# A hybrid attention and convolution layer: each modulation block's product in one group of sixteen matmuls, four weight buffers, and a reordered stage list

## The chip, the cores and the metric

The kernel runs on one core of a Trainium2 chip. The metric is the device time of one execution in microseconds (us). Three runs of the kernel before gave 747.54, 747.73 and 748.13 us, a median of 747.73.

The engines are named as in the profile: PE (TensorE, matmuls and transposes; PEld its weight loads), DVE (VectorE), ACT (ScalarE), POOL (GpSimd) and SP (the engine that issues nearly all the transfers).

## The reference

One layer of a diffusion model for 128 context tokens and 512 latent tokens (640 in all), model width 1024, all in float32:

```
mod = silu(cond) @ w_ada + b_ada            # (1, 6 * 1024): sh1, sc1, g1, sh2, sc2, g2
h = rms(x, norm_mix) * (1 + sc1) + sh1
q, k, v, gb, gc, u = split(h @ w_in)        # 512, 128, 128, 512, 512, 512 columns
attn   = softmax attention, 8 q heads, 2 kv heads, head size 64, rotary positions;
         latent queries see all 640 keys, context queries the 128 context keys
y_conv = gb * conv3(gc * u)
x = x + g1 * (concat(rms(attn), rms(y_conv)) @ w_out)
h2 = rms(x, norm_ffn) * (1 + sc2) + sh2
x = x + g2 * ((silu(gate) * up) @ w_down)   # gate, up = h2 @ w_gate_up, width 2816
```

There are two conditions: `c` for the latent tokens and `c_ctx` for the context tokens. Outputs are x of both kinds of token and k and v of the context tokens.

## The kernel before

Large products keep float32 accuracy by splitting each operand into a high and a low part (names ending in h and l or H and L) and summing three products: high by high, high by low, low by high. Activations are held with the contraction on partitions, 8 tiles of 128.

The program has four stages: the opening (norms, first modulation, the input projection), which ends near 80 us; attention together with the convolution's products, to about 251 us; the output projection with the second norm, to about 300 us; and the feed-forward part to the end.

**The stage list.** In the second stage the string `SEQ` sets the order in which steps are written out, and on PE, ACT, DVE and SP instructions run in that order but for small priorities. The entries are: `k`, `K`, `q`, `Q` (split, then turn a tile's keys or queries; `kv_mm`, `k_turn`, `q_split`, `q_turn`), `a`, `t`, `o` (scores, turn and output of context attention), `Sn.h`, `Tn.g`, `On.g` (`att_s`, `att_t`, `att_o`: scores, turn, and output of unit n, of 16), `r` (an rms), and `F1`, one piece of the filler.

A unit's scores (L835) go into one PSUM buffer "s". DVE takes their maximum (nsr L841), ACT the exponential (pr L845), and one of the two halves is scaled on ACT (L849), the other on DVE. PE then turns them (L862) and multiplies by v (L879). After two units of a head group, `att_add` sends the 64 partitions that must change place through two transfers (es, L894 and L895, 64 KB in all) and adds what comes back on DVE (of, L900 and L901).

**The filler.** Its 84 pieces are 72 convolution pieces and 12 modulation pieces, one modulation piece after every six convolution pieces. A convolution product (`conv_mm`, L723 to L725) accumulates 8 tiles in three pieces of nine matmuls for each half of the 640 tokens. Its PSUM buffer is one of three with the tag "c", which the modulation shares.

**The modulation.** The columns of `w_ada` for g1, sh2 and sc2 are six blocks of 512 (`ADA`). For each, `cond_mm` (L394) multiplies eight tiles of the condition by the weights; tile k writes the 32 PSUM partitions k % 4, so four tiles run side by side. The sum over the four is made later: for sh2 and sc2 by four transposes (L446) and a reduction (modt L448), for g1 by a matmul with `selT` (L785). One `cond_mm` is two instructions in the profile. The two lines between which a piece ends are

```
if h == 1:
    yield
```

so a block is two pieces with four products each, and the transposes of one block stand at the start of the next block's first piece, or, for the last block, in the out-projection. Weights of a block come in four loads of 512 KB (aw) into two buffers (`AWB`). `W` issues the next loads as soon as their buffers are free, in one order with all other weights (wf), on SP.

**The output projection** begins with the context tile's products (ph L155 to L157) behind the last entry of `SEQ`. Two lines of work on DVE run in it: wl L252 scales and splits w_out, aacc L1041 and L1043 forms the last modulation, g2.

Of the kernel before, what the change touches and what calls it, by code (L numbers as in the profile page):

```python
# [37 lines left out]
XB = 3  # L38
SEQ = ('c0 k1 q4 k4 C0 k0 K4 Q4 a0 q0 F1 k2 K0 a1 t0 k3 t1 K1 o0 F1 Q0 o1 K2 K3 q1 F1 S0.0 F1 F1 F1 S0.1 F1 '
# [10 lines left out]
GCUT = [0, 6, 12, 17, 22]  # L50
GB = 3
SOP = [20, 0]
# [20 lines left out]
BPL = 1500  # L73
AP0 = 60
MXP = [300, 200, 0, 0, 0]
AWB = 2
AO = 6
SOON = 150
SOW = -300
# [12 lines left out]
def build(ctx, tc, x_prompt, x_sample, c, cache_k, cache_v, c_ctx, norm_mix, norm_ffn, w_ada, b_ada,  # L92
# [27 lines left out]
    def T(tag, shape, dt=F32, bufs=1):  # L120
        seq[0] += 1
        return pools[where.get(tag, "A")][1].tile(list(shape), dt, tag=tag, bufs=bufs, name=f"{tag}_{seq[0]}")

    def PB(shape=(P, 512), dt=F32, tag="t"):
        seq[0] += 1
        if kept.get(tag):
            w = kept[tag].pop()
            n = 1
            for y in shape[1:]:
                n *= y  # L130
            w = w[:, :n] if tag != "s" else w
            if tag != "s" and len(shape) > 2:
                names = "abc"[:len(shape) - 1]
                w = w.rearrange("p (" + " ".join(names) + ") -> p " + " ".join(names), **dict(zip(names, shape[1:])))
            return w
        return pools["psum"][1].tile(list(shape), dt, tag=tag, bufs=pbufs[tag], name=f"p{tag}_{seq[0]}")
# [10 lines left out]
    def early(n):  # L147
        return tc.high_priority(n)
# [72 lines left out]
    def load(e, later=False):  # L221
# [4 lines left out]
        a, b = src.shape[1], src.shape[2]  # L226
        wf = T("aw", (P, a, b), F32, AWB) if ring == "a" else T("wf", (P, a, b), F32, WFB)
        sp.dma_start(wf, src)
# [30 lines left out]
    def W(key):  # L259
        p = place[key]  # L260
        while not in_pre[0] and stream_at[0] < len(order):
            nxt = order[stream_at[0]][0][0]
            ahead = AO if nxt == "o" else AOP if nxt in ("g", "u", "op") else AHEAD
            if stream_at[0] > p + ahead or order[stream_at[0]][2] > phase[0]:
                break
            load_next()
        assert order[p][5] is not None, key
        return order[p][5]
# [123 lines left out]
    def cond_mm(out, k, w):  # L392
        g = k % 4
        pe.matmul(out[CG * g:CG * (g + 1)], cp[:, k], w, start=(k < 4), stop=(k >= KD - 4), skip_group_check=True)  # L394
# [16 lines left out]
    def mod_evict(i, f0, n, ps_sc, ps_sh):  # L411

        no = (V_MIX, V_FFN)[i]
        bo = (0, 24)[i]
        if ps_sc is not None:
            tmp = ps_sc
            dve.tensor_tensor(tmp, ps_sc, vec[:, no + f0:no + f0 + n].unsqueeze(2).to_broadcast([P, n, 2]), ALU.mult)
            dve.tensor_tensor(modA[i][:, f0:f0 + n, :], tmp,
                              nb[:, i, f0:f0 + n].unsqueeze(2).to_broadcast([P, n, 2]), ALU.add)
        if ps_sh is not None:  # L420
            dve.tensor_tensor(modB[i][:, f0:f0 + n, :], ps_sh,
                              vec[:, bo + f0:bo + f0 + n].unsqueeze(2).to_broadcast([P, n, 2]), ALU.add)
# [19 lines left out]
    def mod_sum(res, n, tag):  # L442

        tp = PB((P, n, P), tag=tag)
        for i in range(n):
            pe.transpose(tp[:, i], res[:, i * P:(i + 1) * P], ident)  # L446
        out = T("modt", (P, n, 2), F32, 2)
        dve.tensor_reduce(out, tp.rearrange("p i (g c) -> p i c g", c=CG)[:, :, 0:2], AX.X, ALU.add)  # L448
        return out
# [317 lines left out]
    def ada_all():  # L767
        for sec, j in ADA:
            rp = PB(tag="c")
            for h in range(4):  # L770
                w = W(("ada", sec, j, h))
                for i in range(2):
                    cond_mm(rp, 2 * h + i, w[:, i])
                if h == 1:
                    yield
            res = T("rs5", (P, 512))
            with early(RSP) if RSP else ExitStack():
                act.activation(res, rp, AF.Copy)
            if sec == 2:
                sp.dma_start(res[2:3], b_ada[0:1, sec * D + j * 512:sec * D + (j + 1) * 512])  # L780
            yield
            if sec == 2:
                for cc in range(2):
                    ps = PB(tag="c")
                    pe.matmul(ps, selT[:, cc], res, start=True, stop=True)  # L785
                    act.activation(g1[cc][:, j * 512:(j + 1) * 512], ps, AF.Copy)
            else:
                ps = mod_sum(res, 4, "c")
                if sec == 4:
                    mod_evict(1, 4 * j, 4, ps, None)  # L790
                else:
                    mod_evict(1, 4 * j, 4, None, ps)

    ada_gen = ada_all()

    def ada_some(n):
# [171 lines left out]
    def rms_of(t):  # L968
        if t == CTX or t >= 0:
# [5 lines left out]
             "a": ctx_s, "t": ctx_t, "o": ctx_o, "r": att_rms}  # L975
    for x in SEQ.split():
        if "." in x:
# [120 lines left out]
    for j in range(2):  # L1098
        cols = slice(j * 512, (j + 1) * 512)
        for n, t in enumerate(TORD):  # L1100
            cc = 1 if t == CTX else 0
            c0 = t * P + (2 if t == CTX else 0)
# [230 lines left out]


tile_hymba = with_exitstack(build)

_INS = ["x_prompt", "x_sample", "c", "cache_k", "cache_v", "c_ctx", "norm_mix", "norm_ffn", "w_ada", "b_ada",
# [44 lines left out]
```

## Time and profile before

| | |
|---|---|
| median of three runs | 747.73 us (747.54 to 748.13) |
| the profiled execution's own time | 747.58 us |
| its span, first to last instruction | 745.8 us |
| mean granted TensorE clock | 0.999 |
| PE busy | 729.5 us, 98% |
| DVE busy | 529.8 us, 71% |
| ACT busy | 375.6 us, 50% |
| transfers | 84.50 MB, 113 GB/s on average |

The own time holds the span and 1.78 us around it. A matmul's busy time overlaps the next one's, so the distance from start to start tells what it costs PE, and a PE that is busy all of a window may still have room. A bracket behind a row of the timeline, [0.95 <-DVE modt L448], gives the idle time before the instruction and whose instruction ended it. The modulation groups (L394, weights aw) run from 94.0 to 249.7 us.

### The profile page before, as it was taken

How to read it: one execution, taken by the hardware profiler on the slowest of the kernel's cores; microseconds unless marked ns; L12 is line 12 of the kernel's file. 1: busy time of each engine (PE TensorE's matmuls, PEld its weight loads, DVE VectorE, ACT ScalarE, POOL GpSimd, SP SyncE). 2: the span in 40 equal slices, each digit the busy share in tenths (PEclk: the TensorE clock that was granted, in tenths of full speed). 3: DMA queues.
4: the chain of work that ended last, by engine and by line, in shares of the span. 5: the costliest groups of instructions: out<-in, count | busy, mean ns of one | idle time of the engine just before them, and what ended most of it. 6: DMA issues, size and time to landing. Idle time of an engine off the chain costs nothing.

```text
span 745.8 us, 11640 instructions
## 1 busy us (share of the span) xinstructions
PE 729.5 (98%) x4556; PEld 657.5 (88%) x4556; DVE 529.8 (71%) x905; ACT 375.6 (50%) x701; POOL 48.6 (7%) x85
## 2 busy tenths in 40 slices
PE   7999899999999999999999999999999999999997
PEld 5568878988998887899998799998899998899986
DVE  5668878685666797888869767864668765677653
ACT  5357877676766544765552135552135541354510
POOL 2403201002010210000000000000000000000000
PEclk9999999999999999999999999999999999999999
DMA  9985133523424363032336314224014132123312
GB/s 288 294 248 165 43 113 104 167 93 117 152 92 147 109 225 114 26 89 57 114 97 195 89 31 112 76 95 142 28 57 113 57 113 86 57 75 96 105 65 85
DMA packets 101387, 84.50 MB, mean 113 GB/s; under 512 B 3502, under 2 KB 81650, under 8 KB 101332
## 3 DMA queue, kind: packets, MB, share of 16 engines
q1 hardware_dynamic: 100980, 83.39, 36.6%
q8 instruction: 36, 0.59, 0.4%
q0 software_dynamic: 352, 0.37, 0.3%
q14 instruction: 19, 0.16, 0.1%
HBM read 79.68 MB, written 2.75 MB: 111 GB/s over the span
## 4 chain that ended last, share of the span: by engine, by line
PE 85%; DVE 6%; DMA 3%; ACT 3%; issue 2%; POOL 1%; SPq 0%; ACTq 0%; DVEq 0%; POOLq 0%
PE pf L155 19%; PE pf L156 19%; PE pf L157 19%; PE pc L723 3%; PE pc L725 3%; PE pc L724 3%; PE pt L862 3%; PE po L879 2%; PE ps L835 2%; PE pc L394 2%; PE ph L156 1%; PE ph L157 1%; PE ph L155 1%; DMA es<-t 1%; DMA af<-in_w_ada_dram 1%
## 5 line engine op out<-in xcount | busy, mean ns | idle before, releaser
L151 ACT ACTIVATE wh<-wf 128x1024 fp32r<-128x1024 f32 (+1 forms) x68 | 65.7, 969 | 107.3 <-PE pf L157 67.0
L152 DVE TENSOR_TENSOR wl<-wf,wh 128x1024 fp32r<-128x1024 f32 (+1 forms) x58 | 69.2, 1195 | 59.2 <-ACT wh L151 45.2
L155 PE MATMUL pf<-B,wh 128*128 128x320 f32 x288 | 89.1, 309 | 0.0
L157 PE MATMUL pf<-B,wl 128*128 128x320 f32 x288 | 89.1, 309 | 0.0
L156 PE MATMUL pf<-B,wh 128*128 128x320 f32 x288 | 89.0, 309 | 0.0
L155 PE MATMUL pf<-wh,gT 128*128 128x512 f32 (+1 forms) x225 | 86.9, 386 | 0.0
L155 PE MATMUL pf<-T,wh 128*128 128x320 f32 x280 | 86.7, 310 | 0.0
L156 PE MATMUL pf<-wl,gT 128*128 128x512 f32 (+1 forms) x225 | 86.5, 385 | 0.0
L156 PE MATMUL pf<-T,wh 128*128 128x320 f32 x280 | 86.5, 309 | 0.0
L157 PE MATMUL pf<-T,wl 128*128 128x320 f32 x280 | 86.5, 309 | 0.0
L157 PE MATMUL pf<-wh,gT 128*128 128x512 f32 (+1 forms) x225 | 86.5, 384 | 0.0
L151 ACT ACTIVATE wh<-sx 128x1024 fp32r<-128x1024 f32 x40 | 42.4, 1060 | 61.7 <-DVE sx L206 22.9
L152 DVE TENSOR_TENSOR wl<-sx,wh 128x1024 fp32r<-128x1024 f32 x40 | 49.0, 1225 | 28.5 <-ACT wh L151 24.9
L723 PE MATMUL pc<-hH,wh 128*128 128x320 f32 x192 | 61.0, 318 | 0.9 <-DVE modt L448 0.9
L725 PE MATMUL pc<-hH,wl 128*128 128x320 f32 x192 | 59.3, 309 | 0.0
L724 PE MATMUL pc<-hL,wh 128*128 128x320 f32 x192 | 59.3, 309 | 0.0
L157 PEld LDWEIGHTS pf<-B,wl 128*128 128x128 f32 x288 | 54.1, 188 | 0.1
L155 PEld LDWEIGHTS pf<-B,wh 128*128 128x128 f32 x288 | 54.1, 188 | 0.1
L156 PEld LDWEIGHTS pf<-B,wh 128*128 128x128 f32 x288 | 54.1, 188 | 0.1
L155 PEld LDWEIGHTS pf<-T,wh 128*128 128x128 f32 x280 | 52.5, 188 | 0.5 <-ACT pf L1241 0.3
L156 PEld LDWEIGHTS pf<-T,wh 128*128 128x128 f32 x280 | 52.6, 188 | 0.0
L157 PEld LDWEIGHTS pf<-T,wl 128*128 128x128 f32 x280 | 52.5, 188 | 0.0
(302 smaller groups left out, 1669.4 us busy)
## 6 DMA issues: line engine op xcount, KB each, us to landing
wf<-in_w_gate_up_dram SPq DMA_DIRECT2D x44, 512.0 KB, 4.1
aw<-in_w_ada_dram SPq DMA_DIRECT2D x24, 512.0 KB, 4.3
wf<-in_w_down_dram SPq DMA_DIRECT2D x20, 512.0 KB, 4.2
wf<-in_w_in_dram SPq DMA_DIRECT2D x18, 512.0 KB, 5.8
af<-in_w_ada_dram SPq DMA_DIRECT2D x32, 256.0 KB, 6.4
x<-in_x_sample_dram SPq DMA_DIRECT2D x8, 512.0 KB, 6.2
wf<-in_w_out_dram SPq DMA_DIRECT2D x8, 512.0 KB, 3.5
wf<-in_w_ada_dram SPq DMA_DIRECT2D x8, 512.0 KB, 3.9
```

The lines of the kernel that those rows point to most:

```text
L151: act.activation(hi, src, AF.Copy)
L152: dve.tensor_tensor(lo, src, f32(hi), ALU.subtract)
L155: pe.matmul(out, lh, rh, start=start, stop=False, skip_group_check=more)
L156: pe.matmul(out, lh, rl, start=False, stop=False, skip_group_check=more)
L157: pe.matmul(out, ll, rh, start=False, stop=stop, skip_group_check=more)
L394: pe.matmul(out[CG * g:CG * (g + 1)], cp[:, k], w, start=(k < 4), stop=(k >= KD - 4), skip_group_check=True)
L723: pe.matmul(acc, wh[:, k], hH[k][:, c0:c0 + n], start=(k == 0), stop=False)
L724: pe.matmul(acc, wh[:, k], hL[k][:, c0:c0 + n], start=False, stop=False)
L725: pe.matmul(acc, wl[:, k], hH[k][:, c0:c0 + n], start=False, stop=(k == KD - 1))
L835: pe.matmul(s2[:, g, :320], q, kk[:, v, P + g * 320:P + (g + 1) * 320], start=(i == 0), stop=(i == 1))
L862: pe.transpose(tp[:, i, h], u[3][h][:, kt * P:(kt + 1) * P], ident)
L879: pe.matmul(ov, w, x[:, i].rearrange("p a q -> p (a q)"), start=(g == 0 and i == 0 and n == 0), stop=(last and i == len(kts) - 1 and n == 1))
```

## The change

A block's modulation product becomes one piece: all eight `cond_mm` and the ACT copy of the result (`rs5`). The turn, or for g1 the two matmuls with `selT`, gets a piece of its own. The pieces stay 84 in number, and 12 of them modulation. `AWB` goes from 2 to 4. In `SEQ`, `K0` moves from before `a1` to behind `o0 F1`, `q1` from before `S0.0` to behind `S0.1 F1`, some thirty others by one to three places, and the last `F1` comes to stand behind `O15.2`. Line numbers from 774 on are smaller by one or two in the changed kernel (L835 becomes L834, L862 L861, L879 L878, L894 L893, L785 L783).

```diff
-SEQ = ('c0 k1 q4 k4 C0 k0 K4 Q4 a0 q0 F1 k2 K0 a1 t0 k3 t1 K1 o0 F1 Q0 o1 K2 K3 q1 F1 S0.0 F1 F1 F1 S0.1 F1 '
+SEQ = ('c0 k1 q4 k4 C0 k0 K4 Q4 a0 q0 F1 k2 a1 t0 k3 t1 K1 o0 F1 K0 Q0 o1 K2 K3 F1 S0.0 F1 F1 F1 S0.1 F1 q1 '
...
-AWB = 2
+AWB = 4
...
     def ada_all():
         for sec, j in ADA:
             rp = PB(tag="c")
             for h in range(4):
                 w = W(("ada", sec, j, h))
                 for i in range(2):
                     cond_mm(rp, 2 * h + i, w[:, i])
-                if h == 1:
-                    yield
             res = T("rs5", (P, 512))
...
                 else:
                     mod_evict(1, 4 * j, 4, None, ps)
+            yield
```

PE at the first group. Names are tile_number; the first block's product is pc_285 before, pc_278 after. Before:

```order
L835 MATMUL ps_282_1246<-KB_169_730,qT_263_1142 128x320 x2
L394 MATMUL pc_285_1258<-aw_179_756,cp_5_85 32x512 x2
L394 MATMUL pc_285_1258<-aw_227_961,cp_5_85 32x512 x2
L723 MATMUL pc_292_1278<-hH0_51_193,wh_165_715 128x320
L724 MATMUL pc_292_1278<-hL0_59_201,wh_165_715 128x320
L725 MATMUL pc_292_1278<-hH0_51_193,wl_166_716 128x320
```

After:

```order
L834 MATMUL ps_275_1229<-KB_169_730,qT_263_1142 128x320 x2
L394 MATMUL pc_278_1241<-aw_179_756,cp_5_85 32x512 x2
L394 MATMUL pc_278_1241<-aw_227_961,cp_5_85 32x512 x2
L394 MATMUL pc_278_1241<-aw_282_1248,cp_5_85 32x512 x2
L394 MATMUL pc_278_1241<-aw_283_1252,cp_5_85 32x512 x2
L723 MATMUL pc_298_1295<-hH0_51_193,wh_165_715 128x320
```

The block's second half, which ran at 112.57 us before, now stands behind its first, ahead of the next scores, S1.0.

PE at the last block's start, near 237 us. pc_675 is the fifth block's turn, pc_677 the sixth block's product, pt_692 a turn of scores. Before:

```order
L725 MATMUL pc_662_3002<-hH7_58_200,wl_605_2731 128x320
L446 MATMUL pc_675_3073<-ident_3_77,rs5_646_2923 128x128 x4
L394 MATMUL pc_677_3082<-aw_644_2915,cp_5_85 32x512 x2
L394 MATMUL pc_677_3082<-aw_645_2919,cp_5_85 32x512 x2
L862 MATMUL pt_692_3123<-ident_3_77,pr_633_2876 128x128
L862 MATMUL pt_692_3123<-ident_3_77,pr_649_2933 128x128
L723 MATMUL pc_695_3130<-hH0_51_193,wh_642_2911 128x320
```

After:

```order
L861 MATMUL pt_674_3070<-ident_3_77,pr_654_2949 128x128
L394 MATMUL pc_677_3082<-aw_611_2748,cp_5_85 32x512 x2
L394 MATMUL pc_677_3082<-aw_612_2752,cp_5_85 32x512 x2
L394 MATMUL pc_677_3082<-aw_678_3083,cp_5_85 32x512 x2
L394 MATMUL pc_677_3082<-aw_679_3085,cp_5_85 32x512 x2
L861 MATMUL pt_693_3129<-ident_3_77,pr_639_2892 128x128
L861 MATMUL pt_693_3129<-ident_3_77,pr_654_2949 128x128
L723 MATMUL pc_696_3136<-hH0_51_193,wh_609_2744 128x320
```

The turn that stood ahead of the group has gone to a place some seventy rows earlier, and the second half of the group has come from behind the last convolution product, some seventy rows later.

SP in the middle of the second stage: L228 a weight load, L894 and L895 (L893 and L894 after) the two transfers of es, t2 what they send. Before:

```order
L895 DMA es_515_2298<-t2_485_2154 64x2x128
L228 DMA aw_530_2375<-in_w_ada_dram 128x2x512
L228 DMA aw_531_2379<-in_w_ada_dram 128x2x512
L228 DMA wf_683_3095<-in_w_out_dram 128x2x512
L894 DMA es_561_2520<-t2_546_2437 64x2x128
```

After:

```order
L228 DMA aw_535_2389<-in_w_ada_dram 128x2x512
L228 DMA aw_536_2393<-in_w_ada_dram 128x2x512
L228 DMA aw_606_2734<-in_w_ada_dram 128x2x512
L228 DMA aw_607_2738<-in_w_ada_dram 128x2x512
L228 DMA wf_683_3095<-in_w_out_dram 128x2x512
L893 DMA es_561_2518<-t2_552_2453 64x2x128
```

Ahead of es_561 stand four loads of a block's weights in place of two.

18 rows, old and new, of the table SEQ are left out of this document.

## The prediction

> **What bounds the kernel now.** I read the page first, for the engine that carries the time. The profiled execution took 747.58 us by its own clock, 745.8 us of it the span, so 1.78 us lie around the span and are taken as unchanged. The median of the three runs is 747.73 us, 0.15 us above the profiled one.
>
> ```profile
> span 745.8 us, 11640 instructions
> PE 729.5 (98%) x4556; PEld 657.5 (88%) x4556; DVE 529.8 (71%) x905; ACT 375.6 (50%) x701; POOL 48.6 (7%) x85
> PE 85%; DVE 6%; DMA 3%; ACT 3%; issue 2%; POOL 1%; SPq 0%; ACTq 0%; DVEq 0%; POOLq 0%
> ```
>
> TensorE (PE) is busy 98% of the span and carries 85% of the chain that ended last. So a change gains in two ways: work taken off PE where PE is the limit, and waits of PE that go away. 0.2% of this time is 1.5 us, about what a measurement of this kernel can tell from no change; faster means below 746.2, slower above 749.2.
>
> Then the waits of PE from 60 to 320 us, the stretch in which the stage list sets the order (us in total, times, longest), and the windows (columns: length, then busy time of PE, PEld, DVE, ACT, POOL, the clock, DMA).
>
> ```profile
> PE pc L723 <- DVE modt L448: 0.9, 1, 0.9
> PE ps L835 <- ACT pr L845: 0.9, 1, 0.9
> PE pt L862 <- ACT pr L849: 0.7, 1, 0.7
> ...
> PE ph L156 <- DVE wl L252: 0.4, 1, 0.4
> 80.00:100.00 20.00, 16.55 (x112) 13.57 (x111) 17.96 (x42) 15.68 (x39) 4.92 (x8) 1.00 0.36 107
> 100.00:120.00 20.00, 19.90 (x149) 18.38 (x148) 14.91 (x29) 14.90 (x33) 0.56 (x1) 1.00 0.31 98
> 220.00:240.00 20.00, 19.05 (x139) 16.85 (x138) 12.53 (x29) 15.33 (x34) 1.75 (x3) 1.00 0.31 95
> 260.00:280.00 20.00, 20.00 (x91) 16.59 (x90) 19.37 (x35) 8.41 (x17) 3.33 (x3) 1.00 0.58 210
> ```
>
> From 80 to 100 us PE idles 3.45 us of 20, and VectorE (DVE) is busy 17.96: the attention starts there, and its softmax chain is the limit. From 100 us PE is full but for one wait, 0.9 us at 239 us. From 260 us DVE is busy 19.37 of 20; PE shows busy too, with 91 longer matmuls, but the chain of waits, further down, runs over DVE: the out-projection is limited by it.
>
> **The change part by part.** *Merging the groups.* Before, each modulation block is two groups of four products (each prints as two PE instructions); after, it is one group of eight. The timeline shows what a group costs beside conv and score matmuls (start, busy time, what, count, wait in brackets):
>
> ```profile
> 93.61 0.46 PE L835 MATMUL ps<-KB,qT 128*128 128x320 f32 x2
> 94.00 1.06 PE L394 MATMUL pc<-aw,cp 128*32 128x512 f32 x8
> 95.00 0.41 PE L723 MATMUL pc<-hH,wh 128*128 128x320 f32 x1
> 95.25 0.30 PE L724 MATMUL pc<-hL,wh 128*128 128x320 f32 x1
> 95.39 0.31 PE L725 MATMUL pc<-hH,wl 128*128 128x320 f32 x1
> ...
> 97.43 0.56 PE L835 MATMUL ps<-KA,qT 128*128 128x320 f32 x2 [0.85 <-ACT pr L845]
> 97.82 0.46 PE L835 MATMUL ps<-KB,qT 128*128 128x320 f32 x2
> 98.11 0.27 PE L862 MATMUL pt<-ident,pr 128*128 128x128 f32 x1
> 99.10 0.55 PE L862 MATMUL pt<-ident,pr 128*128 128x128 f32 x3 [0.71 <-ACT pr L849]
> ...
> 112.57 1.06 PE L394 MATMUL pc<-aw,cp 128*32 128x512 f32 x8
> L394 PE MATMUL pc<-aw,cp x96: 592/605/617, 94.0 to 249.7; 128*32 128x512 f32 x96
> ```
>
> Into the group: two KB scores take 0.39 to the next start (93.61 to 94.00) where they usually take 0.29 (97.82 to 98.11), so 0.10 is lost. Inside: 1.00 from 94.00 to 95.00. Out: the first conv matmul takes 0.25 to the next start and the following one 0.14, so about 0.10 more. A group of four costs 0.10 + 1.00 + 0.10 = 1.20. Its eight records run in two rounds; the whole is 1.06 and one record 0.605 (the last row, min/median/max in ns), so the second round starts 0.455 behind the first. A group of eight has two rounds more: 1.00 + 2 × 0.455 = 1.91, and 2.11 with entry and exit. Two groups of four cost 2.40, so a merge saves 0.29, and six save 1.7 us of PE time. The bounds: 0.1 each, where only the entry goes, to 0.3.
>
> The 0.10 in and 0.10 out are the row's price of going from full-width matmuls to 32-column ones and back. The Trainium skill, "TensorEngine Tiling (Array Packing)", section "Key Properties", says that changing the tiling mode drains TensorE, while changing the tile alone does not. Read as a full tail on both sides, that is 0.31 − 0.14 = 0.17 in and 0.605 − 0.455 = 0.15 out, an estimate that would raise a merge from 0.29 to 0.32; no row here shows so much, and the rows' 0.29 is used.
>
> How much of the 1.7 reaches the end? The end follows the last conv product, because everything behind it hangs on DVE:
>
> ```profile
> 249.20 1.06 PE L394 MATMUL pc<-aw,cp 128*32 128x512 f32 x8
> 250.20 0.38 PE L879 MATMUL po<-ph,VS 128*128 128x256 f32 x1
> ...
> 252.58 0.48 ACT rs L778
> 254.00 3.93 DMA es<-t
> 257.95 0.42 DVE of L901
> 285.26 0.67 DVE wl L252
> ```
>
> (The last four are from the chain of waits.) Before, the twelfth group runs behind the last conv product. After, all groups lie ahead of it. Up to that point 11 groups of four, 13.20 us, become six groups of eight, 12.66 us: **−0.5 us**. The 1.20 that goes behind it lets PE reach the out-projection earlier, where it then waits for DVE; I count it at nothing (at most −1.2, if DVE has slack there; the chain shows one DVE operation after another to 285.26). The last turn moves from the out-projection to just before it: same PE time on either side, and at most its 0.6 busy time lies differently.
>
> *The group ahead of S1.0.* The second half of the first block, 1.00 − 0.09 = 0.91 of PE work, moves from 112.57 to 95.0, ahead of the S1.0 scores, which waited 0.85 for the exp (97.43). The wait covers it: S1.0 starts when it did, and the work is gone from 112.57, where PE was full. That work is the same 0.91 that the −0.5 has counted against (six whole blocks in place of five and a half), so the 0.85 of cover is a gain of its own: **−0.85 us**. If the softmax chain hands the delay on (T0.0 waits 0.71 for the normalised scores, which an earlier S1.0 does not bring sooner) it is 0; if T0.0's wait also goes, −1.6.
>
> *The stall at 239 us.*
>
> ```profile
> 236.32 0.60 PE L446 MATMUL pc<-ident,rs 128*128 128x128 f32 x4
> 236.85 1.06 PE L394 MATMUL pc<-aw,cp 128*32 128x512 f32 x8
> 237.84 0.44 PE L862 MATMUL pt<-ident,pr 128*128 128x128 f32 x2
> 239.23 0.39 PE L723 MATMUL pc<-hH,wh 128*128 128x320 f32 x1 [0.95 <-DVE modt L448]
> 237.62 0.42 DVE L900 TENSOR_TENSOR of<-t,es 64x256 f32<-64x256 f32 x1 [0.98 <-DMA es<-t]
> 239.00 0.18 DVE L448 TENSOR_REDUCE modt<-pc 128x8 f32<-128x32 f32 x1
> ```
>
> Turn, group and conv product each take one of three PSUM buffers "c", the group's product is held over two pieces, and the conv product needs the turn's buffer, read only at 239.00 because DVE sat 0.98 behind the transfer es. After, the turn stands half a block away and the group's buffer is free at once, so a conv product finds a buffer older by one. **−0.95 us**; 0 if the buffer that it then needs is read as late by the same delayed DVE.
>
> *K0, q1 and the other entries.* K0 goes behind o0, q1 behind S0.1: their operations on DVE move by a few places in its own order, and DVE is full there either way (17.96 of 20). No row prices a reordering; 0, with the wait of S1.0, 0.85, as the bound both ways. Moves of one to three places between 112 and 235 us land where PE waits for nothing: 0.
>
> *Four weight buffers.* Loads come in fours behind each group instead of in pairs. Twelve groups from 94.0 to 249.2 us are 14.1 apart, so a whole block's weights are needed 28 us after the last block's, and a load takes 4.3 (row below). At nothing: the wait that the loads had is covered by 28 us. What falls into such a burst is the rival below.
>
> The sum: −0.5 − 0.85 − 0.95 = −2.3 us, 747.6 − 2.3 = **745.3 us**.
>
> **The rivals.** *Waits only move (B).* The softmax chain takes the 0.85 back and the conv product at 239 us waits for another late DVE read. For it: DVE's 17.96 of 20 at the start, and the es wait itself remains. Against it: PE is full from 100 us on, so nothing there can take it back. Left is −0.5: 747.1 us, within 0.2%.
>
> *Transfers es are caught behind the weight bursts (C, slower).* The rows (KB each, us to landing; then DVE's waits from 60 to 320 us):
>
> ```profile
> aw<-in_w_ada_dram SPq DMA_DIRECT2D x24, 512.0 KB, 4.3
> es<-t SPq DMA_DIRECT2D x20, 64.0 KB, 2.1
> DVE of L900 <- DMA es<-t: 2.2, 4, 1.0
> ```
>
> All are issued by one queue (SP). DVE works in order and stands at L900 until es has landed; softmax and conv reads queue behind it, as at 239 us, where one late transfer cost PE 0.95. In the order after, an es pair stands inside a burst of four or behind it, with at most one other load between, in three places. If each lands as late as the slowest es in the rows, 3.93 instead of 2.1, that is 1.8 each, 5.4 in all: 747.6 − 2.3 + 5.4 = 750.7 us. It decides if an es pair is issued before the burst ahead of it has drained. At 210 GB/s (window 260 to 280) four loads, 2.1 MB, take 10 us. Against it: most of L900's waits were hidden, 2.2 us in four, and only one reached PE. The Trainium skill, "DMA: Bandwidth & Descriptors", section "Queues, rings and completion order", states a rule against this change: one issuing engine has one ring on each DMA engine, and descriptors are consumed in ring order. By it every es so placed would be late; the rows agree in so far as landings differ (2.1 and 3.93), but none shows an es behind four loads.
>
> *The gain is larger (D).* The whole 1.7 of the merges counts, and both early waits and the one at 239 us vanish: −1.7 − 1.6 − 0.95 = −4.2, 743.4 us. It needs slack on DVE after 250 us, which the 19.37 of 20 speaks against.
>
> *The change does not do what it says:* were the groups to keep two entries each, by reordering or a wait for the third buffer between, twelve prices of 1.20 stand against eleven, the first term is +1.2 and the sum 1.2 − 0.85 − 0.95 = −0.6: 747.0 us, counted with B.
>
> **How the numbers follow.** The forecast with its bounds (744.3, with T0.0's wait gone and part of the 1.2, to 746.2, with the 0.85 taken back) 0.53; B 0.14; C in full 0.18, in part 0.06; D 0.09. The likeliest gives 745.3. C in part is one late es pair in place of three, 747.1, or two, 748.9. The range must leave out no more than 0.2: from 743.3, with D, to 749.0, with B and C in part; C in full, 0.18, is left out. Faster by over 0.2% are the forecast and D: 0.62. Within 0.2%: B and C in part: 0.20. Slower: C in full, 0.18.
>
> **What would show it.** Right: the group of sixteen records from entry to exit near 1.9 us; no wait, or a small one, at the S1.0 scores; no wait of a conv product for modt in 220 to 250 us; the last conv product about 2.3 us earlier, and the out-projection's last DVE operation too. Wrong: PE waits for DVE where DVE waits for es behind weight loads (C); the waits of 60 to 112 us as large in sum as before (B); the last conv product earlier but the end not, so that the out-projection gave it back; the end earlier by more than the last conv product (D).

## The result and the profile after

Over 20 runs each, the changed kernel took a median of 746.57 us (745.97 to 747.37), the kernel before 748.35 us. The ratio is 0.9974, with a 95% interval of 0.9967 to 0.9981: faster by 0.26%, about 1.9 us. The forecast was 2.3 us.

The page of the changed kernel:

```profile
span 745.2 us, 11646 instructions
PE 729.4 (98%) x4556; PEld 658.8 (88%) x4556; DVE 530.3 (71%) x905; ACT 375.1 (50%) x701; POOL 49.0 (7%) x85
PE 84%; DVE 6%; DMA 4%; ACT 3%; issue 1%; POOL 1%; SPq 0%; ACTq 0%; DVEq 0%; POOLq 0%
```

The page alone hardly shows the change: the span is 0.6 us shorter, not 1.9. This execution took 747.05 us, 0.5 above the median of its kernel, and the one before 747.58, 0.8 below its own. A second profile of the changed kernel (an experiment below) has a span of 744.2. So the places are compared, not the spans. The waits of PE from 60 to 320 us:

```profile
PE pt L935 <- DVE pr L929: 0.9, 1, 0.9
PE ps L834 <- DVE KB L670: 0.7, 1, 0.7
PE pt L703 <- ACT qT L704: 0.7, 1, 0.7
PE ph L156 <- DVE wl L252: 0.6, 2, 0.4
PE ps L834 <- ACT pr L844: 0.6, 1, 0.6
PE po L878 <- DVE pl L152: 0.5, 1, 0.5
```

The wait of a conv product for modt (0.9) and that of T0.0 for pr (0.7) are gone, the wait of scores for the exp is 0.6 in place of 0.9. New are 0.5 for pl, in the last unit, and 0.4 more for KB. By windows:

```profile
80.00:100.00 20.00, 17.95 (x129) 14.84 (x128) 18.27 (x44) 16.64 (x43) 4.30 (x9) 1.00 0.37 109
100.00:120.00 20.00, 19.33 (x135) 17.66 (x135) 14.48 (x29) 15.10 (x33) 0.56 (x1) 1.00 0.38 118
220.00:240.00 20.00, 20.00 (x149) 18.37 (x149) 13.95 (x31) 14.67 (x31) 0.55 (x1) 1.00 0.13 37
260.00:280.00 20.00, 20.00 (x90) 16.54 (x89) 18.81 (x30) 9.27 (x19) 2.59 (x2) 1.00 0.50 164
```

PE does 1.40 us more in 80 to 100 us (17.95 against 16.55), and it is busy throughout from 220 to 240, where it idled 0.95 before. From 260 to 280 us DVE is a little less full (18.81 in place of 19.37). The two places that the prediction spoke of, in the timeline:

```profile
94.40 0.46 PE L834 MATMUL ps<-KB,qT 128*128 128x320 f32 x2
94.78 1.92 PE L394 MATMUL pc<-aw,cp 128*32 128x512 f32 x16
96.64 0.42 PE L723 MATMUL pc<-hH,wh 128*128 128x320 f32 x1
96.89 0.31 PE L724 MATMUL pc<-hL,wh 128*128 128x320 f32 x1
...
98.06 0.46 PE L834 MATMUL ps<-KA,qT 128*128 128x320 f32 x2
...
101.27 0.56 PE L834 MATMUL ps<-KA,qT 128*128 128x320 f32 x2 [0.56 <-ACT pr L844]
...
235.12 1.92 PE L394 MATMUL pc<-aw,cp 128*32 128x512 f32 x16
236.97 0.44 PE L861 MATMUL pt<-ident,pr 128*128 128x128 f32 x2
237.17 0.39 PE L723 MATMUL pc<-hH,wh 128*128 128x320 f32 x1
```

A group of sixteen records takes 1.86 from start to next start (94.78 to 96.64) where 1.91 was reckoned. S1.0 (98.06) no longer waits; S1.1 (101.27), which did not wait before, waits 0.56. The conv product behind the last group waits for nothing.

The table cuts the executions at places that all kernels pass: the start of the scores S0.0, of S3.0, of the last conv matmul, of the first feed-forward matmul (pf on B), of the first one on T, and of the last matmul. It is in us, each figure the difference of two starts in the timeline of PE.

| | S0.0 to S3.0 | to the last conv | to the feed-forward | to T | to the end | sum |
|---|---|---|---|---|---|---|
| before | 22.53 | 137.32 | 65.39 | 31.01 | 396.66 | 652.91 |
| changed | 22.57 | 134.83 | 66.01 | 31.69 | 396.79 | 651.90 |
| changed, again | 22.45 | 134.84 | 66.03 | 31.50 | 396.43 | 651.26 |
| grouping, old list | 23.25 | 135.65 | 65.81 | 31.08 | 396.62 | 652.40 |
| old groups, new list | 22.73 | 136.91 | 65.58 | 31.02 | 396.62 | 652.86 |
| before, four buffers | 22.39 | 137.23 | 65.77 | 31.01 | 396.74 | 653.15 |
| changed, K0 and q1 back | 22.90 | 134.85 | 66.02 | 31.03 | 397.38 | 652.17 |
| turn at the group | 22.37 | 136.32 | 65.67 | 31.03 | 396.70 | 652.09 |
| first block only | 22.91 | 136.19 | 67.03 | 31.03 | 396.78 | 653.94 |
| one more group behind conv | 22.66 | 134.83 | 66.05 | 31.03 | 396.82 | 651.38 |
| one more group at S8.0 | 22.63 | 136.01 | 65.94 | 31.14 | 396.96 | 652.69 |
| last group behind conv | 22.89 | 132.88 | 66.74 | 31.03 | 396.80 | 650.34 |
| last group behind O15.2 | 22.73 | 132.98 | 67.17 | 31.01 | 396.52 | 650.41 |

Each row is one execution. Two of the same PE order (before, and before with four buffers; the changed kernel twice) differ by up to 0.4 in a column. In the first column, eight executions whose order up to S3.0 is that of the changed kernel (changed, again, both with one more group, turn at the group, first block only, both with the last group moved) spread from 22.37 to 22.91, so a difference of 0.5 there is not read as an effect.

### The profile page after: what moved, and what is told of

Same layout as the page of the kernel before. It is cut to its first block, busy times and chain, and to the rows that moved or that the text cites. A ratio compares the mean times of both kernels' runs of the same rounds, so it can differ in the third digit from the quotient of the medians.

```text
span 745.2 us, 11646 instructions
## 1 busy us (share of the span) xinstructions
PE 729.4 (98%) x4556; PEld 658.8 (88%) x4556; DVE 530.3 (71%) x905; ACT 375.1 (50%) x701; POOL 49.0 (7%) x85
## 4 chain that ended last, share of the span: by engine, by line
PE 84%; DVE 6%; DMA 4%; ACT 3%; issue 1%; POOL 1%; SPq 0%; ACTq 0%; DVEq 0%; POOLq 0%
PE pf L155 17%; PE pf L156 17%; PE pf L157 17%; PE pc L723 4%; PE pc L724 4%; PE pc L725 4%; PE po L878 3%; PE ps L834 3%; PE pt L861 2%; PE pc L394 2%; PE ph L156 2%; PE ph L157 2%; PE ph L155 2%; DMA wf<-in_w_gate_up_dram 2%; DMA af<-in_w_ada_dram 1%
```

## The experiments

All ratios are against the kernel before on the same chip, with 95% intervals.

**The two parts alone.** The grouping with the old list, and the new list with the old grouping:

```diff
 # the changed kernel, with
-SEQ = (the changed list)
+SEQ = (the list of before)
```

> The changed kernel (one group of sixteen per block, four weight buffers) with the stage list of before. Theory G (the grouping brings the gain): all three terms stay, so 1.9 to 2.7 us below before, and the scores S0.0 wait 0.3 for KB, as before, in place of 0.7. Theory L (the moved list entries bring it, the grouping nothing): within 0.7 us of before. Theory S (both are needed, the list was fitted to the grouping): 0.5 to 1.5 below before, with new waits of PE between 100 and 250 us.

```diff
 # the kernel before, with
-SEQ = (the list of before)
+SEQ = (the changed list)
```

> The kernel before (two groups of eight matmuls per block, two weight buffers) with the changed stage list. Theory G: the 0.85 wait of S1.0 and the stall of a conv product near 239 us remain or move, and the moved K0 and q1 cost the 0.4 us that the trace of the changed kernel shows at S0.0: 0 to 0.7 us above before. Theory L: 1.5 to 2.3 us below before.

Measured: 747.43 us, 0.9995 (0.9986 to 1.0003), and 747.82 us, 0.9994 (0.9984 to 1.0004). Neither part alone can be told from no change; together they bring 0.9974. That is theory S, though just under its size (0.46 us below before, where it said 0.5 to 1.5). The table says where: to the last conv matmul the grouping with the old list gains 0.95 (158.90 against 159.85), the new list alone 0.21, both together 2.45. With the old list, S0.0 to S3.0 takes 0.72 longer than before, since the second half of the first group is hidden hardly at all there:

```profile
PE pt L861 <- ACT pr L848: 0.7, 1, 0.7
PE ps L834 <- ACT pr L844: 0.6, 1, 0.6
```

T0.0 still waits 0.7 (waits of PE, 60 to 320 us, grouping with the old list); the 0.6 of S1.1 stands in the changed kernel too. From S3.0 to the last conv product the grouping with the old list loses another 0.8 against the changed kernel (135.65 against 134.83). Half of it is one place: behind the third group, a turn of scores starts 0.94 behind the last record of the group instead of 0.52, after a wait of 0.35 for DVE's pl.

**The buffers.**

```diff
 # the changed kernel, with
-AWB = 4
+AWB = 2
```

> The changed kernel with two weight buffers in place of four. The second half of a block's weights can then be sent for only when the first half has been read. Theory G: PE waits in the middle of each of the six groups for a load, about 4.3 us from issue to landing each: 20 to 30 us above before. Rival (the buffers do nothing, the loads come early enough): within 0.5 us of the changed kernel.

```diff
 # the kernel before, with
-AWB = 2
+AWB = 4
```

> The kernel before with four weight buffers and nothing else changed. Theory G: within 0.7 us of before, since the loads were landed in time. Theory B (earlier loads bring the gain by emptying the queue for the transfers es): 1 to 2 us below before, and the wait of DVE for es near 238 us shorter.

Measured: 789.99 us, 1.0564 (1.0547 to 1.0581), and 747.65 us, 0.9993 (0.9984 to 1.0002). Four buffers show no effect of their own, but the grouping needs them. The size was missed: 42 us above before, not 20 to 30. The waits of PE, its timeline, and windows of 4 us around the first group, with two buffers:

```profile
PE pc L394 <- DMA aw<-in_w_ada_dram: 26.1, 6, 5.6
94.63 1.07 PE L394 MATMUL pc<-aw,cp 128*32 128x512 f32 x8
100.41 3.34 PE L394 MATMUL pc<-aw,cp 128*32 128x512 f32 x8 [4.71 <-DMA aw<-in_w_ada_dram]
94.00:98.00 4.00, 1.70 (x13) 0.60 (x11) 4.00 (x7) 2.81 (x6) 0.91 (x2) 0.96 0.68 175
98.00:102.00 4.00, 1.59 (x6) 0.37 (x8) 1.15 (x2) 1.19 (x2) 0.00 (x0) 0.50 0.98 326
102.00:106.00 4.00, 4.00 (x19) 2.34 (x16) 0.00 (x0) 0.60 (x1) 0.00 (x0) 0.69 0.61 186
```

Six waits make 26.1 us, as expected. Then the half group takes 3.34 in place of 1.07: its last load is still on its way, and the granted clock (last but two of a window's columns) is 0.50, then 0.69. The Trainium skill, "TensorE: Matmul & The Clock Gate", section "What's actually happening", says that an idle window of about 3.4 us halves the clock and a busy one brings it back. The rows agree on the half (0.50) and on its return, but not on the length: the 0.96 of the window from 94 to 98 us puts the fall 0.3 us before its end (an estimate, with the clock either 1 or 0.5), only about 2.0 us after PE's last record ended at 95.70.

**K0 and q1.** The changed kernel run again, and with these two entries at their old places:

> The changed kernel itself, run again on the same chip as the kernels beside it. Theory N (the 0.8 us that the first trace of it lost between the start of the feed-forward part and its second tile is one late weight load of that run): the stretch from the first feed-forward matmul to the first one on T takes 31.0 us as before, not 31.7, and the end is earlier by it. Theory P (it belongs to the change): 31.7 again.

```diff
-... F1 k2 a1 t0 k3 t1 K1 o0 F1 K0 Q0 o1 K2 K3 F1 S0.0 F1 F1 F1 S0.1 F1 q1 ...
+... F1 k2 K0 a1 t0 k3 t1 K1 o0 F1 Q0 o1 K2 K3 q1 F1 S0.0 F1 F1 F1 S0.1 F1 ...
```

> The changed kernel with K0 and q1 of the stage list back at their old places, all else as changed. Theory G as first told (K0 and q1 cost 0.4 and bring nothing): 0.2 to 0.6 us below the changed kernel. Theory Q (q1 behind S0.1 is what lets the group's second half hide in the wait of S1.0, as the stage list of before with the grouping lost 0.7 from S0.0 to S3.0): 0.3 to 0.9 us above the changed kernel, with the waits of S1.1 and T0.0 back at 0.6 and 0.7.

Measured: 746.27 us, 0.9976 (0.9966 to 0.9985), and 746.66 us, 0.9981 (0.9973 to 0.9990). The medians stand 0.4 us apart the way theory Q says, but the intervals overlap. What the trace shows is a wait that changes its place. With K0 and q1 at their old places:

```profile
PE pt L861 <- ACT pr L848: 0.7, 1, 0.7
PE ps L834 <- ACT pr L844: 0.6, 1, 0.6
PE ps L834 <- DVE KB L670: 0.3, 1, 0.3
```

T0.0 (the first row) waits 0.66 again; in the eight executions with the changed order there it waits 0.29 at most. S1.1 (the second) waits 0.56 in all of them, so theory Q was wrong to expect that wait to come back: it had not gone. In return, S0.0 waits less for KB, 0.3 in place of 0.5 to 0.8. From S0.0 to S3.0 it takes 22.90, at the upper end of those eight (22.37 to 22.91), so a net gain of K0 and q1 is not shown. The 0.7 that the first trace lost ahead of T (31.69 against 31.01) is 0.5 again here, and 0 to 0.1 in the other kernels made from it (31.03 with the group behind conv). It was not settled whether the change has a part in it.

**The free place behind the last conv product, and the price of a group.** A group of eight records whose result is not used, on weights that are there already (wkeep), at two places:

```diff
+    def extra_group():
+        xp = PB(tag="c")
+        for i in range(4):
+            pe.matmul(xp[CG * i:CG * (i + 1)], cp[:, i], wkeep[i // 2][:, i % 2], start=True, stop=True, skip_group_check=True)
...
+            if x == "O15.0":    # in the other kernel "S8.0"
+                extra_group()
```

> The changed kernel with one more group of eight 32-column matmuls behind O15.0, that is behind the last convolution product; its result is not used. Theory G (from there on VectorE sets the time, so that the group of before that stood there cost nothing at the end): the out-projection begins 1.2 us later and the end within 0.4 us of the changed kernel. Rival D (PE sets the time there too): the end 1.2 us later.

> The changed kernel with one more group of eight 32-column matmuls behind S8.0, where PE waits for nothing; its result is not used. Theory G: the last convolution product 1.2 us later and the end 0.7 to 1.2 us later. Rival (a group between other matmuls costs only its own columns, without entry and exit, or is hidden): 0 to 0.6 later.

Measured: 746.26 us, 0.9978 (0.9969 to 0.9986), the same as the changed kernel's 746.27 beside it; and 747.43 us, 0.9994 (0.9986 to 1.0003), 1.16 us more. A group of four products costs its 1.2 in the middle, and nothing behind O15.0. The out-projection then begins 0.2 later behind the last conv product (2.88 against 2.68), not 1.2 as expected. The changed kernel, then the one with the added group there:

```profile
247.67 0.38 PE L878 MATMUL po<-ph,VS 128*128 128x256 f32 x1
248.52 0.39 PE L878 MATMUL po<-pl,VS 128*128 128x256 f32 x1 [0.47 <-DVE pl L152]
248.74 0.60 PE L446 MATMUL pc<-ident,rs 128*128 128x128 f32 x4
...
249.97 0.28 PE L886 MATMUL po<-ph,VS 128*128 128x256 f32 x1
250.09 0.28 PE L886 MATMUL po<-pl,VS 128*128 128x256 f32 x1
250.21 0.60 PE L446 MATMUL pc<-ident,rs 128*128 128x128 f32 x4
```

In the last unit PE waits for pl. The wait shows as 0.47 of idle time, but from start to start it costs about 1.0: the last product before it stands 0.26 behind its forerunner, the next ones 0.85 and 0.22, where 0.12 each is usual. The added group fills that wait, and the starts are 0.12 apart again.

**The turn beside the group.**

```diff
             yield
+            yield
             if sec == 2:
...
                     mod_evict(1, 4 * j, 4, None, ps)
-            yield
```

> The changed kernel with each block's turn (or its two matmuls with selT) back at the start of the next block's piece, directly ahead of the next group of sixteen, and an empty piece where it was. Theory G (the conv product near 237 us waits because turn and group, side by side, leave it the buffer that VectorE reads last): a wait of a conv product for modt of 0.5 to 1.2 us comes back in one place or more, and the end is 0.5 to 1.2 us above the changed kernel. Theory L (the moved list entries took that wait away, by letting the transfer es land in time): no such wait, within 0.4 us of the changed kernel.

Measured: 747.16 us, 0.9990 (0.9981 to 0.9999), 0.6 and 0.9 us above the changed kernel's medians, which come from other sets of runs (the intervals of the ratios meet at 0.9981 to 0.9985), but not by the wait that was expected. No conv product waits for modt. PE around the last group, and DVE, of this kernel:

```profile
235.78 0.60 PE L446 MATMUL pc<-ident,rs 128*128 128x128 f32 x4
236.31 1.92 PE L394 MATMUL pc<-aw,cp 128*32 128x512 f32 x16
238.16 0.44 PE L861 MATMUL pt<-ident,pr 128*128 128x128 f32 x2
238.36 0.39 PE L723 MATMUL pc<-hH,wh 128*128 128x320 f32 x1
237.12 0.42 DVE L899 TENSOR_TENSOR of<-t,es 64x256 f32<-64x256 f32 x1 [0.95 <-DMA es<-t]
238.02 0.19 DVE L448 TENSOR_REDUCE modt<-pc 128x8 f32<-128x32 f32 x1
```

DVE waits 0.95 for es, as before, and reads the turn at 238.02. The longer group lasts until 238.16, so that the conv product, at 238.36, finds the buffer free. The loss is elsewhere: 136.32 from S3.0 to the last conv, 1.48 more than the changed kernel. About 1.0 of it stands in three places, where PE waits for the softmax chain, the longest of them

```profile
173.19 0.56 PE L834 MATMUL ps<-KA,qT 128*128 128x320 f32 x2 [0.34 <-ACT pr L844]
```

The scores start here 0.65 behind the conv matmul before them, a turn at 196.98 starts 0.40 and the scores at 224.59 start 0.30 behind the instruction before them, where 0.15, 0.15 and 0.03 are usual. Why the softmax chain is late there was not traced.

**The first block alone.**

```diff
 # the kernel before with the changed list and AWB = 4
-                if h == 1:
+                if h == 1 and blk not in (0, 9):
                     yield
...
+            if blk in (0, 9):
+                yield
```

> The changed stage list and four weight buffers, with only the first block's product in one group of sixteen and its turn in a piece of its own; the other five blocks as before in two groups of eight. Theory G (the second half of the first group hides in the wait of the softmax chain, 0.85 of it): S0.0 to S3.0 takes 22.5 us as in the changed kernel, not 23.4, the last conv product is 1.2 us earlier than in the run of the changed list with all groups old, and the end 0.4 to 1.2 us below before. Rival (the cover is no gain of its own; all of the gain is the later merges): the end within 0.4 us of before.

Measured: 748.91 us, 1.0016 (1.0008 to 1.0025): slower, against both theories. S0.0 to S3.0 takes 22.91 where 23.6 would stand if the 0.91 were not hidden (22.73 of the new list with old groups, and 0.91): 0.7 is hidden. Most of the loss comes at the end:

```profile
251.98 1.07 PE L394 MATMUL pc<-aw,cp 128*32 128x512 f32 x8
254.46 0.50 PE L155 MATMUL ph<-wh,m 128*128 128x512 f32 x1 [1.41 <-ACT rs L778]
```

The changed list puts its last piece behind O15.2. With the last block in two halves that piece is a group, and the out-projection, whose PSUM is laid out anew, waits for ScalarE to copy its result. To the feed-forward it took 67.03, 1.4 more than with the same list and two buffers, where this wait does not show. Why it is 1.4 here is open.

**A version from these runs.** The last block's group goes to the free place, its turn back into the out-projection; one kernel puts the group between O15.0 and O15.1, the other behind O15.2.

```diff
         for sec, j in ADA:
+            if (sec, j) == ADA[-1]:
+                yield
...
-T15.0 T15.1 O14.2 F1 F1 T15.2 F1 O15.0 O15.1 O15.2 F1
+T15.0 T15.1 O14.2 F1 F1 T15.2 F1 O15.0 F1 O15.1 O15.2
```

(The second line only in the first of the two.)

> The changed kernel with the last block's group of sixteen between O15.0 and O15.1, behind the last conv product, an empty piece at its old place, and its turn in the out-projection as before. Theory G (1.2 us of PE work is free behind the last conv product, as the run with an added group there shows): the last conv product 2.0 us earlier, the out-projection 0.9 to 1.3 us earlier, and the end 0.5 to 1.5 us below the changed kernel. Rival (VectorE, which bounds the out-projection, does not start earlier, or the list loses its fit): within 0.4 us of the changed kernel or above it.

> As the run with the last block's group of sixteen between O15.0 and O15.1, but with that group behind O15.2. Theory G: the ScalarE copy of the group's result then stands behind the copy that the last transfer es waits for, so the same or 0.1 to 0.5 us below that run. Rival: the group delays the first product of the out-projection in full, 0.3 or more above that run.

Measured: 745.33 us, 0.9960 (0.9948 to 0.9972), and 745.76 us, 0.9965 (0.9954 to 0.9976). The first is the fastest kernel of this study, about 1 us below the changed one's medians (746.57 and 746.27), which come from other sets of runs; the intervals of the ratios overlap a little (0.9967 to 0.9972). The last conv product comes 2.0 earlier, as expected, and the wait for the copy takes part of it back:

```profile
245.44 1.92 PE L394 MATMUL pc<-aw,cp 128*32 128x512 f32 x16
249.35 0.50 PE L155 MATMUL ph<-wh,m 128*128 128x512 f32 x1 [1.08 <-ACT rs L778]
```

The second, with the group behind O15.2, was not better: its wait for the copy is shorter (0.72), but the out-projection begins 5.06 behind the last conv product, not 4.62.

## Why the prediction was right

The ratio applied to the profiled execution gives 0.9974 × 747.58 = 745.6 us; 745.3 was forecast. By its steps:

- **The price of a group.** Reckoned 1.20 for four products and 2.11 for eight. Measured: 1.16 to 1.2 by the added group, and 0.09 + 1.86 + 0.10 = 2.05 by the trace. Right.
- **Cover ahead of S1.0**, −0.85. From S0.0 to S3.0 the changed kernel does 0.91 more and takes 22.57 and 22.45 against 22.53: 0.9 is hidden, and 0.5 to 1.1 in the eight executions with its order. Right in size, but the reason was half told. S1.0's wait goes in every kernel with the first block in one group and four buffers, with the old list too: from S0.1 to S1.0 it takes 3.95 to 4.10, where it took 4.11 without the 0.91. What the list decides is the step behind it. There S1.1 now waits 0.56, and with the old list T0.0's wait of 0.7 stays as well, so that S1.0 to S1.1 takes 4.10 in place of 3.37 (3.94 with only K0 and q1 back) and only 0.2 is hidden in all: the softmax chain hands the delay on, the case in which the prediction put the gain at 0. In the changed kernel T0.0's wait is gone and the step takes 3.22 and 3.31 (up to 3.57 in the eight). The entries that do this were costed at nothing.
- **From S3.0 to the last conv product:** ten groups become five, 12.00 − 10.55 = 1.45, and the stall, 0.95: 2.40. Measured 2.49 and 2.48. Right.
- **The stall at 239 us** went, but the step named only one of several reasons. In the changed kernel DVE reads the turn at 225.75, half a block ahead of the last group, as the step said. But the stall also goes with the turn left beside the group, where the longer group covers DVE's late read, with the grouping on the old list, and with the new list alone: none of their waits shows a conv product waiting for modt. "Entries moved by one to three places: 0" was wrong so far: without the moved entries the grouping gains 0.95 to the last conv product and not 2.45.
- **Behind the last conv product: nothing gained or lost.** That a group there costs nothing is shown. The reason was in part another: the out-projection does not begin earlier behind the last conv product (2.68 against 2.52), since the wait for pl and the last turn (0.36) have taken the place of the group. But from there to the feed-forward the changed kernel takes 66.0 against 65.4 and 65.8 of the two executions of the old order: 0.2 to 0.6 are given back, which the sum left out. It is lost inside the out-projection: its last wl on DVE starts at 283.70 and 283.29 after 285.18, 1.5 and 1.9 earlier, the last conv product 2.1 and 2.5 earlier. The chain that ended last goes over es and DVE there in the kernel before, over PE's products ph until about 274 us in both executions of the changed one, and over DVE in the one with the added group, whose stretch is as long (66.05): the two paths are about equal, and es stands in neither. What gives the 0.2 to 0.6 back was not settled.
- **Rival C** did not come. DVE's waits for es from 60 to 320 us in the changed kernel:

```profile
DVE of L899 <- DMA es<-t: 1.8, 4, 0.6
DVE of L900 <- DMA es<-t: 0.6, 3, 0.3
...
aw<-in_w_ada_dram SPq DMA_DIRECT2D x24, 512.0 KB, 6.3
es<-t SPq DMA_DIRECT2D x20, 64.0 KB, 2.1
...
209.45 1.40 SPq L228 DMA_DIRECT2D aw<-in_w_ada_dram  x3
213.84 0.60 SPq L893 DMA_DIRECT2D es<-t  x1
```

That is 2.4 us in all (2.2 and 0.2 before), and the longest is 0.6, not 1.0. (Each of the two transfers of es is 64 KB, 128 KB for a pair.) In their bursts the weight loads land later (6.3 us in place of 4.3, the medians), but es lands in 2.1 as before. The last two rows, of SP's timeline, show the nearest pair, 4.4 us behind the start of three loads. The burst had not drained: its second and third load landed at about 214.6 and 216.1, and es at 216.3, 2.4 us after its issue. So the condition of rival C came true at this place, and its price was 0.3 us (2.4 against 2.1), not 1.8. The Trainium skill ("DMA: Bandwidth & Descriptors", section "Queues, rings and completion order") has the rule that descriptors are consumed in ring order. An es that lands 0.2 us behind the loads ahead of it agrees with that but does not show it, since es took 3.0 at 233.65 with no load issued in the 6 us before it.

The miss in the parts is that they were added up as if they stood alone. Grouping and list alone bring nothing at the end that can be told from no change, both together 1.9. That the sum came out so near is in part luck: from S0.0 to the last conv product 2.45 and 2.56 were gained where 2.3 was reckoned, and 0.2 to 0.6 of it, put at nothing, was lost behind.

## What to carry to other kernels

Work moved into a wait is free only if what releases the wait does not depend on it and the order around it leaves no second wait right behind; so a regrouping and the order list have to be changed and measured together, and a part that shows nothing alone may still be needed. Before a gain on the busiest engine is counted, add a dummy of the same cost at the place in question: here the same group cost 1.2 us in the middle and nothing behind the last conv product, where it filled a wait, and that pointed to a faster kernel. A single profiled execution can be off its kernel's median by as much as such a change brings; compare distances between fixed places instead of spans.

## What was not expected of the hardware

A wait of 4.7 us for a load cost PE more than its length: the granted clock fell to 0.50, about 2 us into the wait, and was still 0.69 on average from 102 to 106 us, PE having restarted at 100.41. With two weight buffers, 26.1 us of such waits in six groups, the half clock behind them and a shorter wait of each group for its last load came to 42 us.

A short idle time in the profile cost PE twice its length: the 0.47 us before the last unit's po cost about 1.0 from start to start.
